# Solve steps queued behind the preceding large matmul, and decay rows loaded and exponentiated later

## The chip, the cores and the metric

The kernel runs on one core of one Trainium2 chip. The metric is the time of one execution on the device in microseconds (us); less is better. Engines: PE (TensorE matmuls; PEld its weight loads), DVE (VectorE), ACT (ScalarE), POOL (GpSimd), and SP (SyncE), which here issues the DMAs.

## The reference

One decoder layer: 512 tokens, width 2048, float32, with two branches side by side. The change concerns the second branch, a gated delta rule with 16 key heads and 32 value heads of 128 numbers each. Cut to what matters:

```python
d_qkv = causal_conv_silu(d_qkv, conv_w)          # 4 taps, per channel
dq, dk = l2_norm(dq), l2_norm(dk)                # per key head
# in chunks of 64 tokens, per value head:
g = jnp.cumsum(g, axis=-1)
decay = jnp.exp(jnp.where(tril, g[..., :, None] - g[..., None, :], -jnp.inf))
L = jnp.where(strict, (k_beta @ k^T) * decay, 0.0)
t_inv = triangular_solve(eye + L, eye)           # 64 x 64, lower
u = t_inv @ v_beta
w = t_inv @ (k_beta * jnp.exp(g)[..., None])
qk = (q @ k^T) * decay
# then a scan over the 8 chunks:
v_new = u_c - w_c @ S
o = qd_c @ S + qk_c @ v_new
S = S * gl_c + kd_c^T @ v_new
```

## The kernel before

**Weights and tiles.** The large projections stream their weights through SBUF as `raw` tiles of 1 MB (two buffers). Each is split by halves into a rounded part `whi` (a cast on ACT, L52) and a rest `wlo` (a subtraction on DVE, L53). A *tile* below is one output tile of 128 channels by 512 tokens: 48 matmuls of 128x512 into one of two PSUM buffers (`mm3`, L223 to L225, called by `channel_tile`). Positions are given in tiles, so tile 29.5 is the middle of tile 29, and a split stands about one half tile ahead of its use at the latest. The branch's tiles come in this order: 0 to 3 merge gates, 4 to 7 keys 4 to 7, 8 to 23 keys 8 to 15 and merge gates in turn, 24 to 30 merge gates, then from 31 on sixteen groups of heads of five tiles each (q, v, v, z, z), group 8 from tile 71.

**Work beside the matmuls.** Everything else of the branch is written as Python generators. After every second k-tile of a channel tile (so eight times per tile) `pump` advances them: the live ones by their delays, and the slow ones by a budget. That is the program order. A scheduler then places the instructions of each engine by its own modelled times, in which the program order is a priority, so an instruction whose operands it takes for ready can stand many tiles ahead of its place in the program. At run time each engine works its list in order and waits at the head of it.

**A key head** (`keys`, two value heads each) runs: convolution (ACT, then three operations on DVE, then tanh `th` on ACT and a product on DVE), transposes `ptk` on PE, sums of squares on ACT (L673), `rsqrt` on DVE in small steps, the norm's products `k` on ACT (L640), transposes `ptkT`, a copy `kT` on ACT (L648), and the key products `pkk` on PE (L655). For each of its two value heads a row block `E` (256 KB, four buffers) is loaded by `decay_load` (L678), masked on POOL (L685, L686), exponentiated on ACT (L650), multiplied with `pkk` on DVE (L658), and stored to `lt_d` and `lab_d`.

**The solves.** `solve` inverts the triangular 64x64 matrices of 16 value heads at once on DVE: solve 0 for the first eight key heads, solve 1 for the others. It loads `A` in two halves of 1 MB and `bet` in two small ones, multiplies `A` by `nbet` (L709), runs 62 steps of two operations each (L717, L723), copies `A` out in four pieces (ACT copy L729, DMA `ta_d` L731), multiplies by `bet` (L733) and stores `ts_d` in two DMAs of 1 MB (L737). In the program solve 0 begins at key 8 and has to end before the first group of heads, solve 1 begins at the first group and ends before group 8. Solve 0's steps are tied in the order behind the latest key's `rsqrt`; solve 1's steps aren't tied to anything.

**A group of heads** (`queries`, `values`, `scan`) loads `E` rows, `kT`, `k`, and blocks of `ts_d`, `ta_d`, `lab_d`, and works through transposes (`ptq`, `ptv`, `pto`), products (`pqk`, `py`, `pu`) and the scan.

Of the kernel before, what the change touches and what calls it, by code (L numbers as in the profile page):

```python
# [2 lines left out]

# [7 lines left out]
AF = mybir.ActivationFunctionType  # L11
# [25 lines left out]
class Layer:  # L37
# [43 lines left out]
    def pump(self):  # L81
        self.weight_tick()
        for e in list(self.live):
            e[1] -= 1
            if e[1] <= 0:
                self.step(e)
        for e in list(self.slow):
            e[2] += e[1]
            while e in self.slow and e[2] >= e[3]:
                e[2] -= e[3]  # L90
                self.step_slow(e)
        for q in list(self.side.values()):
            if not q:
                continue
            q[0][2] += q[0][1]
            while q and q[0][2] >= 1.0:
                q[0][2] -= 1.0
                if next(q[0][0], True):
                    q.pop(0)

    def step(self, e):
        try:
            e[1] = next(e[0]) or 1
        except StopIteration:
            self.live.remove(e)
# [114 lines left out]
    def mm3(self, ps, w, x, first, last):  # L220
        nc = self.nc
        (wh, wl), (xh, xl) = w, x
        nc.tensor.matmul(ps, lhsT=wh, rhs=xh, start=first, stop=False)  # L223
        nc.tensor.matmul(ps, lhsT=wh, rhs=xl, start=False, stop=False)  # L224
        nc.tensor.matmul(ps, lhsT=wl, rhs=xh, start=False, stop=last)  # L225

    def channel_tile(self, name, xh=None, xl=None):

# [395 lines left out]
    def keys(self, wk, g, ps):  # L624

        nc = self.nc
        y = wk.tile([P, T], F32, tag="y", name="y", bufs=3)
        yield from self.conv(wk, ps, 16 + g, y)
        E = [self.decay_load(wk, 2 * g + e) for e in range(2)]
        yield 2  # L630
        pt = self.ptp.tile([P, T], F32, tag="tp", name="ptk")
        self.transpose4(pt, lambda c: y[:, c * P : (c + 1) * P])
        ss = self.sumsq(wk, pt)
        yield 3
        nc.vector.tensor_scalar(out=ss, in0=ss, scalar1=EPS, scalar2=None, op0=ALU.add)
        rk = self.rsqrt(wk, ss, NTB, "rk")
        yield 2
        k = wk.tile([P, NTB, P], F32, tag="k", name="k")
        for c in range(NTB):
            nc.scalar.activation(k[:, c, :], pt[:, c * P : (c + 1) * P], AF.Copy, scale=rk[:, c : c + 1])  # L640
        for e in range(2):
            self.decay_mask(E[e], 2 * g + e)
        yield 3
        pt = self.ptp.tile([P, T], F32, tag="tp", name="ptkT")
        self.transpose4(pt, lambda c: k[:, c, :])
        nc.sync.dma_start(out=self.k_d[g], in_=k.rearrange("p c d -> p (c d)"))
        kT = wk.tile([P, T], F32, tag="kT", name="kT")
        nc.scalar.copy(out=kT, in_=pt)  # L648
        for e in range(2):
            nc.scalar.activation(E[e], E[e], AF.Exp)  # L650
        yield 2
        pk = self.ptp.tile([P, NTB, P], F32, tag="tp", name="pkk")
        for c in range(NTB):
            sl = slice(c * P, (c + 1) * P)
            nc.tensor.matmul(pk[:, c, :], lhsT=kT[:, sl], rhs=kT[:, sl], start=True, stop=True)  # L655
        nc.sync.dma_start(out=self.kT_d[g], in_=kT)
        for e in range(2):
            nc.vector.tensor_tensor(out=E[e], in0=pk, in1=E[e], op=ALU.mult)  # L658
        yield 2
        for e in range(2):  # L660
            h = 2 * g + e
            b, hl = h // 16, h % 16
# [13 lines left out]
    def decay_load(self, wk, h):  # L676
        E = wk.tile([P, NTB, P], F32, tag="E", name="E", bufs=4)
        self.nc.sync.dma_start(out=E.rearrange("p c i -> p (c i)"), in_=self.g_rows[h].partition_broadcast(P))  # L678
        return E
# [840 lines left out]
```

## Time and profile before

| | us |
|---|---|
| median of 3 runs | 2965.86 (2963.03 to 2968.37) |
| profiled execution | 2968.14 |
| its span on the core | 2964.4 |
| PE busy | 2882.8 (97%) |
| DVE busy | 1786.1 (60%) |
| ACT busy | 1086.6 (37%) |
| POOL busy | 236.2 (8%) |

The profile is of one execution. A row of a timeline is: start in us, duration in us, engine, line of the kernel, operation, output and inputs, and in brackets how long the engine had been idle and what ended that. A row of the waits is: who waited, for whom, us in total, times, and the longest. The granted clock of PE is 1.00 at full speed and 0.50 at half.

### The profile page before, as it was taken

What the parts mean: (1) busy time and instruction counts of PE and PEld (TensorE: products, weight loads), DVE (VectorE), ACT (ScalarE), POOL (GpSimd) and SP (SyncE); (2) the same over time, 40 slices, a digit from 0 to 9 for tenths busy, and PEclk for the clock granted to TensorE, in tenths of its full rate; (3) what the DMA queues carried; (4) which work ended last, traced back from release to release, by engine and by line L of the source; (5) the groups of instructions that cost most, each with busy time, mean ns of one, the idle gap of its engine ahead of it and who ended that gap; (6) DMA issues with size and microseconds to landing.
All of it is one profiled execution on the core that took longest, in us unless ns stands there. A gap on an engine that the chain in (4) does not pass through costs nothing.

```text
span 2964.4 us, 38028 instructions
## 1 busy us (share of the span) xinstructions
PE 2882.8 (97%) x14556; PEld 2362.5 (80%) x14556; DVE 1786.1 (60%) x2903; ACT 1086.6 (37%) x2105; POOL 236.2 (8%) x204
## 2 busy tenths in 40 slices
PE   8899999999999999999999999999999999999988
PEld 6687777777888888888888878888788788788877
DVE  7755979998544445454545453433755655554697
ACT  4354433334333333334333322311244434432343
POOL 0012210111000000011000000000100000000013
PEclk9999999999999999999999999999999999999999
DMA  9756555634433333333332575554322223375553
GB/s 382 278 159 189 173 151 156 181 115 123 151 108 122 108 122 115 125 124 116 123 123 86 197 265 193 201 167 162 100 86 98 79 88 107 111 257 174 178 199 96
DMA packets 174023, 451.11 MB, mean 152 GB/s; under 512 B 72177, under 2 KB 74737, under 8 KB 138129
## 3 DMA queue, kind: packets, MB, share of 16 engines
q1 hardware_dynamic: 173842, 448.70, 45.7%
q8 instruction: 114, 1.87, 0.3%
q14 instruction: 67, 0.55, 0.1%
HBM read 386.95 MB, written 59.45 MB: 151 GB/s over the span
## 4 chain that ended last, share of the span: by engine, by line
PE 81%; DVE 9%; DMA 4%; ACT 2%; issue 2%; POOL 1%; SPq 0%; POOLq 0%; DVEq 0%; ACTq 0%
PE mm L223 23%; PE mm L225 22%; PE mm L224 22%; DVE wlo L53 2%; DMA E<-g_rows 1%; DVE wa L396 1%; PE S L1160 1%; PE po L890 1%; PE pv L871 1%; PE O L1211 1%; DVE A L723 1%; PE pP L257 1%; DVE atmp L717 1%; ACT whi L52 1%; PE pd L886 1%
## 5 line engine op out<-in xcount | busy, mean ns | idle before, releaser
L223 PE MATMUL mm<-hh,whi 128*128 128x512 f32 x2784 | 1135.8, 408 | 7.0 <-DVE yq L561 6.2
L225 PE MATMUL mm<-hh,wlo 128*128 128x512 f32 x2784 | 1093.7, 393 | 0.0
L224 PE MATMUL mm<-hl,whi 128*128 128x512 f32 x2784 | 1091.3, 392 | 0.0
L53 DVE TENSOR_TENSOR wlo<-raw,whi 128x1024 fp32r<-128x1024 f32 (+1 forms) x452 | 548.6, 1216 | 491.6 <-ACT whi L52 476.6
L52 ACT CAST whi<-raw 128x1024 fp32r<-128x1024 f32 (+1 forms) x452 | 470.8, 1043 | 951.7 <-PE mm L224 907.0
L223 PEld LDWEIGHTS mm<-hh,whi 128*128 128x128 f32 x2784 | 526.6, 189 | 117.4 <-issue 15.0
L225 PEld LDWEIGHTS mm<-hh,wlo 128*128 128x128 f32 x2784 | 525.5, 189 | 114.3
L224 PEld LDWEIGHTS mm<-hl,whi 128*128 128x128 f32 x2784 | 527.3, 189 | 99.9 <-issue 0.8
L223 PE MATMUL mm<-oh,whi 128*128 128x512 f32 x512 | 200.4, 393 | 1.2 <-ACT whi L52 0.9
L224 PE MATMUL mm<-ol,whi 128*128 128x512 f32 x512 | 199.3, 390 | 0.8 <-DVE ol L53 0.8
L225 PE MATMUL mm<-oh,wlo 128*128 128x512 f32 x512 | 199.4, 390 | 0.5 <-DVE wlo L53 0.5
L818 POOL TENSOR_TENSOR qe<-qe,yq 128x512 f32<-128x512 f32 x32 | 47.3, 1495 | 912.7 <-DMA qe<-eg_rows 848.9
L685 POOL TENSOR_TENSOR E<-E,neg_g 128x512 f32<-128x512 f32 x64 | 76.6, 1197 | 490.9 <-DMA E<-g_rows 427.7
L223 PEld LDWEIGHTS mm<-oh,whi 128*128 128x128 f32 x512 | 96.0, 188 | 23.0 <-ACT whi L52 1.3
L224 PEld LDWEIGHTS mm<-ol,whi 128*128 128x128 f32 x512 | 96.1, 188 | 22.3 <-DVE ol L53 1.2
L225 PEld LDWEIGHTS mm<-oh,wlo 128*128 128x128 f32 x512 | 96.1, 188 | 21.0 <-DVE wlo L53 1.2
L717 DVE TENSOR_TENSOR atmp<-A 128x392 f32<-128x392 f32 (+30 forms) x124 | 108.1, 877 | 2.0
L723 DVE TENSOR_TENSOR A<-A,atmp 128x392 f32<-128x392 f32 (+30 forms) x124 | 108.0, 876 | 2.0
L864 DVE SCALAR_TENSOR_TENSOR r<-pp,neg_eg,vt 128x128 f32<-128x128 f32 x96 | 29.2, 346 | 81.5 <-PE pp L861 79.8
L561 DVE SCALAR_TENSOR_TENSOR yv<-mm,convh,yv 128x511 f32<-128x511 f32 (+2 forms) x96 | 71.3, 743 | 8.2 <-ACT yv L558 6.8
L1184 ACT ACTIVATE sm<-sm,mx,rs 128x256 f32<-128x256 f32 (+1 forms) x128 | 71.7, 562 | 3.3 <-DVE mx L1179 3.3
L224 PE MATMUL m<-wlo,hh 128*128 128x512 f32 x128 | 51.4, 401 | 7.9 <-DVE wlo L53 7.8
(331 smaller groups left out, 3154.9 us busy)
## 6 DMA issues: line engine op xcount, KB each, us to landing
raw<-in_w_ch SPq DMA_DIRECT2D x158, 1024.0 KB
wa<-in_w_ada_ss SPq DMA_DIRECT2D x32, 1024.0 KB
raw<-in_w_od SPq DMA_DIRECT2D x32, 1024.0 KB
E<-g_rows SPq DMA_DIRECT2D x64, 256.0 KB
gw<-in_w_ada_gate SPq DMA_DIRECT2D x16, 1024.0 KB
raw<-in_w_os SPq DMA_DIRECT2D x16, 1024.0 KB
qe<-eg_rows SPq DMA_DIRECT2D x32, 256.0 KB
o_d<-zh SPq DMA_DIRECT2D x32, 256.0 KB
```

Of the source, the lines that this page charges most:

```text
L52: self.nc.scalar.copy(out=hi, in_=src)
L53: self.nc.vector.tensor_tensor(out=lo, in0=src, in1=hi.bitcast(F32), op=ALU.subtract)
L223: nc.tensor.matmul(ps, lhsT=wh, rhs=xh, start=first, stop=False)
L224: nc.tensor.matmul(ps, lhsT=wh, rhs=xl, start=False, stop=False)
L225: nc.tensor.matmul(ps, lhsT=wl, rhs=xh, start=False, stop=last)
L257: self.nc.tensor.transpose(dst[:, c * P : (c + 1) * P], src_cols(c), self.ident)
L561: nc.vector.scalar_tensor_tensor(out=y[:, s:], in0=ps[:, : T - s], scalar=w[:, j : j + 1], in1=y[:, s:], op0=ALU.mult, op1=ALU.add)
L685: nc.gpsimd.tensor_tensor(out=E, in0=E, in1=ng, op=ALU.add)
L717: eng.tensor_tensor(out=t, in0=A[:, m : m + 1, m + 1 :].to_broadcast([P, m, n]), in1=A[:, :m, m : m + 1].to_broadcast([P, m, n]), op=ALU.mult,
L723: eng.tensor_tensor(out=A[:, :m, m + 1 :], in0=A[:, :m, m + 1 :], in1=t, op=ALU.add)
L818: nc.gpsimd.tensor_tensor(out=qf, in0=qf, in1=q, op=ALU.mult)
L1184: nc.scalar.activation(t, t, AF.Exp, scale=r[:, h : h + 1], bias=mx[:, h : h + 1], accum_out=den[:, h : h + 1])
```

## The change

Two things are changed. Every instruction that a solve step issues in `pump` gets an edge to the last large matmul before it in the program, so the scheduler can't place it ahead of that matmul. The edge sets the order only, and no engine waits for it at run time; it holds for a step's DMAs and ACT copies as for its DVE operations. And a key head loads its two `E` blocks after the `rsqrt` is issued instead of after the convolution, and the exps are issued after the key products instead of after the copy `kT`, with one more pump between them and the multiplication.

```diff
     def pump(self):
...
-        for e in list(self.slow):
-            e[2] += e[1]
-            while e in self.slow and e[2] >= e[3]:
-                e[2] -= e[3]
-                self.step_slow(e)
+        with self.behind():
+            for e in list(self.slow):
+                e[2] += e[1]
+                while e in self.slow and e[2] >= e[3]:
+                    e[2] -= e[3]
+                    self.step_slow(e)
...
+    @contextmanager
+    def behind(self):
+
+        n, last = len(self.nc.cur_bb.bb.instructions), self.last_mm
+        yield
+        for i in self.nc.cur_bb.bb.instructions[n:]:
+            self.tc.add_manual_dep(
+                i, last.name, mybir.DependencyInfo(mybir.DependencyClass.NoSync, mybir.DependencyReason.DATA),
+                reason="behind",
+            )
...
-        nc.tensor.matmul(ps, lhsT=wl, rhs=xh, start=False, stop=last)
+        self.last_mm = nc.tensor.matmul(ps, lhsT=wl, rhs=xh, start=False, stop=last).ins
...
     def keys(self, wk, g, ps):
...
         yield from self.conv(wk, ps, 16 + g, y)
-        E = [self.decay_load(wk, 2 * g + e) for e in range(2)]
         yield 2
...
         rk = self.rsqrt(wk, ss, NTB, "rk")
+        E = [self.decay_load(wk, 2 * g + e) for e in range(2)]
         yield 2
...
         nc.scalar.copy(out=kT, in_=pt)
-        for e in range(2):
-            nc.scalar.activation(E[e], E[e], AF.Exp)
         yield 2
...
         nc.sync.dma_start(out=self.kT_d[g], in_=kT)
+        for e in range(2):
+            nc.scalar.activation(E[e], E[e], AF.Exp)
+        yield 1
         for e in range(2):
             nc.vector.tensor_tensor(out=E[e], in0=pk, in1=E[e], op=ALU.mult)
```

Line numbers of the changed kernel are higher by 12 or 13 from here on (L52 and L53 stay). In the order, PE's and POOL's lists are nearly the same as before; those of DVE, ACT and SP move. Three places follow.

DVE before, from the cast of tile 32's second half to the end of the convolutions at tile 33, where the next matmuls wait for `yq` (A and atmp are solve 1's here; solve 0 is over):

```order
L53 TENSOR_TENSOR wlo<-raw,whi 128x1024
L723 TENSOR_TENSOR A<-A,atmp 128x21x42
L717 TENSOR_TENSOR atmp<-A 128x902
L561 SCALAR_TENSOR_TENSOR yq<-mm,convh,yq 128x511
L723 TENSOR_TENSOR A<-A,atmp 128x22x41
L561 SCALAR_TENSOR_TENSOR yq<-mm,convh,yq 128x510
L561 SCALAR_TENSOR_TENSOR yv<-mm,convh,yv 128x511
L561 SCALAR_TENSOR_TENSOR yq<-mm,convh,yq 128x509
```

DVE after, the same place:

```order
L53 TENSOR_TENSOR wlo<-raw,whi 128x1024 x4
L746 TENSOR_TENSOR A<-A,bet 128x4096
L53 TENSOR_TENSOR wlo<-raw,whi 128x1024
L721 TENSOR_SCALAR nbet<-bet 128x64
L573 SCALAR_TENSOR_TENSOR yq<-mm,convh,yq 128x511
L722 TENSOR_TENSOR A<-A,nbet 128x4096
L573 SCALAR_TENSOR_TENSOR yq<-mm,convh,yq 128x510
L723 MEMSET A 128x64
L573 SCALAR_TENSOR_TENSOR yq<-mm,convh,yq 128x509
```

Solve 0's last product (L746) now stands here, at tile 32.2, and was at tile 31.3; solve 1 begins here, with `nbet` and `A` times `nbet` between the operations of `yq`, where before it was at its twenty-second step.

SP before, in the same stretch, from the third piece of solve 0 on (`ta_d`, `ts_d` are solve 0's results):

```order
L731 DMA ta_d<-atmp 64x1024
L183 DMA raw<-in_w_ch 128x2048
L731 DMA ta_d<-atmp 64x1024
L249 DMA ma_d<-mth 128x512
L737 DMA ts_d<-A 64x4096 x2
L183 DMA raw<-in_w_ch 128x2048
L678 DMA E<-g_rows 128x512 x2
L779 DMA kT<-kT_d 128x512
```

SP after:

```order
L712 DMA A<-lt_d 64x4096
L744 DMA ta_d<-atmp 64x1024
L715 DMA bet<-b_rows 64x64
L712 DMA A<-lt_d 64x4096
L744 DMA ta_d<-atmp 64x1024
L750 DMA ts_d<-A 64x4096 x2
L715 DMA bet<-b_rows 64x64
L195 DMA raw<-in_w_ch 128x2048
L691 DMA E<-g_rows 128x512 x2
L792 DMA kT<-kT_d 128x512
```

Solve 1's loads, which stood at tile 2 (`bet`) and at tiles 26 and 27 (`A`), now stand between solve 0's stores, and the second `bet` and the next `raw` stand behind both `ts_d`.

ACT before, at keys 10 and 11 (tiles 14 and 15):

```order
L246 ACTIVATE mth<-mm 128x512
L650 ACTIVATE E<-E 128x512 x2
L640 ACTIVATE k<-ptk,rky 128x128 x4
L52 CAST whi<-raw 128x1024
L650 ACTIVATE E<-E 128x512 x2
L648 COPY kT<-ptkT 128x512
```

ACT after:

```order
L258 ACTIVATE mth<-mm 128x512
L652 ACTIVATE k<-ptk,rky 128x128 x4
L52 CAST whi<-raw 128x1024
L668 ACTIVATE E<-E 128x512 x4
L660 COPY kT<-ptkT 128x512
```

The exps of both keys now stand in one row ahead of the copy `kT`, on which the key products wait, and the products `k` no longer stand behind two of them.

More of the change, by code (lines that the diff above doesn't have):

```diff
@@ L1 @@
 import math
-from contextlib import ExitStack, nullcontext
+from contextlib import ExitStack, contextmanager, nullcontext
 import concourse.bass as bass
```

## The prediction

> **What bounds the kernel now.** I read the page first, then the busy time of each engine by stage, then what PE waits for, and last the timelines around the waits that the change can reach.
>
> ```profile
> span 2964.4 us, 38028 instructions
> PE 2882.8 (97%) x14556; PEld 2362.5 (80%) x14556; DVE 1786.1 (60%) x2903; ACT 1086.6 (37%) x2105; POOL 236.2 (8%) x204
> PE 81%; DVE 9%; DMA 4%; ACT 2%; issue 2%; POOL 1%; SPq 0%; POOLq 0%; DVEq 0%; ACTq 0%
> ```
>
> PE is busy for 2882.8 of 2964.4 us, and it holds 81% of the chain that ended last. The matmuls themselves aren't touched. So the change can only move the 81.6 us in which PE is idle, and the stretches in which PE runs at a lower granted clock. The next view gives, by stage, the window, then the sum, then the busy time of PE, its weight loads, DVE, ACT and POOL, then the granted clock.
>
> ```profile
> 300.00:480.00 180.00, 166.19 (x756) 135.61 (x755) 155.19 (x224) 68.42 (x152) 32.77 (x32) 0.97 0.51 156
> 480.00:720.00 240.00, 230.06 (x1121) 190.55 (x1119) 227.68 (x318) 84.29 (x152) 24.95 (x19) 0.98 0.49 146
> 780.00:1050.00 270.00, 270.00 (x1429) 224.78 (x1428) 134.21 (x253) 100.47 (x224) 24.53 (x24) 1.00 0.37 119
> ```
>
> PE loses 13.8 us while the keys and solve 0 run (DVE 86% busy) and 9.9 us while solve 1 runs (DVE 95% busy). It loses nothing after that (DVE 50% busy). The waits of PE say for what:
>
> ```profile
> PE ptk L257 <- DVE y L568: 11.3, 5, 3.4
> PE ptkT L257 <- ACT k L640: 10.2, 5, 5.5
> PE mm L223 <- DVE yq L561: 6.2, 1, 6.2
> PE pto L257 <- DVE osb L920: 3.9, 2, 3.7
> PE pu L836 <- DMA lab<-lab_d: 2.8, 1, 2.8
> PE ptv L257 <- DVE yv L568: 1.3, 1, 1.3
> ```
>
> The first two are the keys, 21.5 us in ten waits. The third is the hand-over from solve 0 to the heads. The last three (3.9 with a small part elsewhere, 2.8, 1.3) fall beside solve 1. The change reaches these places and no others, and it may open new waits beside them.
>
> **Part 1: the decay rows.** No instruction is added or removed: 32 loads of 256 KB, 32 masks on POOL, 32 exps on ACT. In the order most loads move by a third of a tile or less, since the scheduler had already placed them late. What changes is which ACT work stands behind an exp. Key 6 is the largest wait of this kind (POOL, ACT, PE, then the window behind it):
>
> ```profile
> 254.72 2.10 POOL L685 TENSOR_TENSOR E<-E,neg_g 128x512 f32<-128x512 f32 x1 [5.00 <-DVE y L561]
> 256.90 0.63 POOL L686 TENSOR_SCALAR_AFFINE_SELECT E<-E 128x512 f32<-128x512 f32 x1
> 249.76 0.63 ACT L650 ACTIVATE E<-E 128x512 f32<-128x512 f32 x1 [3.23 <-POOL E L686]
> 257.56 0.63 ACT L650 ACTIVATE E<-E 128x512 f32<-128x512 f32 x1 [5.15 <-POOL E L686]
> 262.59 1.14 ACT L640 ACTIVATE k<-ptk,rky 128x128 f32<-128x128 f32 x4 [2.94 <-DVE rky L64]
> 263.01 1.25 PE L257 MATMUL ptkT<-ident,k 128*128 128x128 f32 x4 [5.47 <-ACT k L640]
> 257.00:275.00 18.00, 12.53 (x56) 10.21 (x55) 10.46 (x28) 10.03 (x24) 4.40 (x5) 0.81 0.46 144
> ```
>
> An exp at 249.76 held back key 6's sums of squares by 3.2 us, and the rsqrt of DVE behind them ended so late that ACT waited another 2.9 us for it. In the new order the sums stand ahead of the exps, and the norm's products stand right behind the exp and th. Counted from the exp at 257.56: 0.6 (exp) + 0.6 (th, an exp's length) + 1.1 (four products) gives about 259.9 against 263.0, so the wait of 5.47 shrinks to about 2.4, a gain of 3.1. The half-speed stretch behind it (18 us at a mean of 0.81, so at most 3.4 us lost, part of which is the idle itself) I take as shortened by 0.9. Of the other 16.0 us of these waits (21.5 less 5.5), keys 9 and 13 to 15 have the same picture with shorter waits; I take a quarter, 4 us. Against that, at keys 10 and 11 the new order puts four exps in a row ahead of the copy kT, on which the key products wait. One mask with its select costs 2.1 + 0.6 us on POOL at worst, so the second key's pair lets kT come about 4 us late where PE waits nearly nothing now. With half clock behind it (1.8), and with key 11's own wait (2.1, one of the five for y) gone, that is 3.7 us lost. The sum is −3.1 − 0.9 − 4 + 3.7, about **−4.5**. The bounds are −11 (all but half of the 21.5 goes) and +4 (only keys 10 and 11 change).
>
> **Part 2: solve 0's end and solve 1's start.** This is the place where tile 33 waits for a free PSUM buffer, which the convolution yq has to read first. Of before, in the order DVE, ACT, SP, POOL, PE:
>
> ```profile
> 530.14 0.26 DVE L723 TENSOR_TENSOR A<-A,atmp 128x62 f32<-128x62 f32 x1
> 548.65 4.43 DVE L733 TENSOR_TENSOR A<-A,bet 128x4096 f32<-128x4096 f32 x1
> 530.44 2.10 ACT L729 COPY atmp<-A 64x1024 f32<-64x1024 f32 x1 [1.24 <-DVE A L723]
> 535.93 2.10 ACT L729 COPY atmp<-A 64x1024 f32<-64x1024 f32 x1 [1.25 <-DMA ta_d<-atmp]
> 555.34 1.05 ACT L52 CAST whi<-raw 128x1024 fp32r<-128x1024 f32 x1 [4.35 <-PE mm L224]
> 560.78 1.06 ACT L52 CAST whi<-raw 128x1024 fp32r<-128x1024 f32 x1 [4.38 <-PE mm L224]
> 553.11 1.09 SPq L737 DMA_DIRECT2D ts_d<-A  x2
> 556.26 0.64 SPq L183 DMA_DIRECT2D raw<-in_w_ch  x1
> 557.00 4.71 SPq L678 DMA_DIRECT2D E<-g_rows  x2
> 564.72 0.32 SPq L779 DMA_DIRECT2D kT<-kT_d  x1
> 569.62 1.82 POOL L685 TENSOR_TENSOR E<-E,neg_g 128x512 f32<-128x512 f32 x1 [104.36 <-DMA E<-g_rows]
> 572.66 0.77 PE L223 MATMUL mm<-hh,whi 128*128 128x512 f32 x1 [6.25 <-DVE yq L561]
> 573.00:576.00 3.00, 3.00 (x8) 2.35 (x8) 3.00 (x5) 0.91 (x2) 2.93 (x3) 0.50 1.14 234
> 303.50 4.42 DVE L709 TENSOR_TENSOR A<-A,nbet 128x4096 f32<-128x4096 f32 x1 [2.77 <-DMA A<-lt_d]
> ```
>
> Solve 0's last step ended at 530.4. Its place in the order moves from tile 29.5 to tile 30.4. The casts at 555.34 and 560.78 belong to tiles 32 and 32.5, half a tile apart, so tile 30.4 is at 560.8 − 2.1 × 10.9 = 538, and the last step ends about there. Each of the four pieces (copy, ta_d) took 5 to 5.5 us; that puts the copies at about 538, 544, 549 and, behind the cast at 555.34 that now stands ahead of it, 556.4 to 558.5. A×bet follows until 562.9, and the two ts_d of 1 MB issue at 563.0 instead of 553.11. On SP the second load of bet (16 KB) now stands directly behind them. On DVE, nbet waits for that load, and behind nbet stand the three yq operations with A×nbet (4.42) and a memset between them. The load's landing is the unknown. Nearest row: the E load issued at 557.00 behind ts_d and a raw had landed only when POOL began at 569.62, 16.5 us after the ts_d issue, and ts_d alone kept SP's load of kT until 564.72, 11.6 us after their issue. So a load behind the two ts_d lands about 11 to 12 us after 563.0, at 574 to 575.3. Then nbet, three yq of 0.7 and A×nbet 4.4 give 7 us: PE starts tile 33 at about 582 against 572.66, **+9.3**. The half clock of the rows at 573 to 576 stands behind both waits and is counted once. The E loads come as much later, and two exps stand ahead of th, which adds at most 3.3 us at the transposes of q; I take 0.7. Sum **+10**. Lower bound: a load that passes the ts_d lands within a few us, and only the order of DVE is left, +1. Upper bound: 9.3 + 3.3 and a raw more in the way, +14. I take the value near the row at 569.62, since both loads are small ones behind the same two stores.
>
> [...]
>
> The two loads of solve 1's A (1 MB each) come into this stretch too, at tiles 31 and 32. They issue before the last ta_d and end before ts_d by the 5.8 us per MB of the two ts_d (11.6 / 2), so they are hidden; without that cover they would add up to a raw's landing, which the upper bound holds.
>
> **Part 3: solve 1 thinned.** Its 62 steps ran beside tiles 27 to 43, and they are now tied to tiles 33 to 60, with the stores at tiles 61 to 66. Its result is read after tile 71, so nothing is late there.
>
> ```profile
> L717 DVE TENSOR_TENSOR atmp<-A 128x392 f32<-128x392 f32 (+30 forms) x124 | 108.1, 877 | 2.0
> 656.00:659.00 3.00, 2.81 (x11) 2.62 (x12) 2.92 (x5) 0.38 (x1) 0.00 (x0) 0.50 0.62 262
> 738.20:743.00 4.80, 4.77 (x25) 3.88 (x26) 4.80 (x2) 2.11 (x3) 0.00 (x0) 0.50 0.33 68
> 728.27 0.48 SPq L731 DMA_DIRECT2D ta_d<-atmp  x1
> 734.74 0.61 SPq L806 DMA_DIRECT2D lab<-lab_d  x1
> 799.28 0.60 PE L257 MATMUL ptv<-ident,yv 128*128 128x128 f32 x4
> 796.91 1.05 DVE L568 SCALAR_TENSOR_TENSOR yv<-th,yv 128x512 f32<-128x512 f32 x1 [2.51 <-ACT th L566]
> ```
>
> A solve costs about 108 us of DVE (L717 for both solves, and the second operation of a step as much again). Over 27 tiles (295 us) that is 37%, on top of the 50% that the heads take alone: 87% instead of 95%. The three waits beside solve 1 cost 3.7 + 2.8 + 1.3 = 7.8 us and half clock for some 3 and 5 us, another 4, so 12 in all. The chain pto (an rsqrt in small DVE steps with solve steps between them) gets half as many steps in its way, and ta_d no longer stands on SP ahead of the lab loads of the same matmul. What remains: in a group without a solve the first ptv starts at 799.28, 1.3 us after its yv is ready (796.91 + 1.05), so one step of 2 × 0.88 us in front of yv makes a wait of about 0.5 us in each of six groups, 3 us; A×bet (4.42) now stands ahead of yv at tile 64.5 and may add 1.5. That makes −12 + 4.5 = **−7.5**, with −12 as the lower end. The upper end is the second rival's, +13.
>
> The sum is −4.5 + 10 − 7.5 = **−2 us**. The profiled run took 2968.14 us (span 2964.4 and 3.7 around it), which is 2.3 above the median of 2965.86. So the run would be at 2966, and the median at about **2964**.
>
> **The rivals.** (a) The load of bet isn't held by the stores: part 2 is +1 and the sum −11, so 2955. The dense DMA after 553 speaks against it, the small size of the load for it. (b) Solve 1 costs in the heads: its steps use up the 1.3 us at the first ptv and more, and each of the six groups waits about 2.4 us. The waits of 2.8, 3.7 and 5.5 us all were followed by half clock, which adds 1.8, so 6 × 4.2 = 25 against the 12 saved: part 3 is +13, the sum +18.5, so 2984. It decides from two or more steps in front of yv. For it speaks that a step follows nearly every half tile there; against it, that in the denser order of before only one of three ptv showed a wait. (c) The new place of the decay rows does nothing, since the scheduler moves them little and the exp still waits for POOL: part 1 is 0, the sum +2.5, 2968.
>
> [...]
>
> **Chances.** Forecast 0.42, (a) 0.16, (b) 0.24, (c) 0.18. About 0.2%, 5.9 us, is what a measurement of this kernel can tell from no change. The forecast's own range is 2956 to 2972, and it splits 0.14 faster, 0.24 same and 0.04 slower. (a) is all faster. (b) is 0.23 slower and 0.01 same. (c) is 0.01 faster, 0.11 same, 0.06 slower. Together: faster 0.31, same 0.36, slower 0.33. The range of 2952 to 2983 takes in (a) and (c) and most of (b).
>
> **What would show it.** Part 1: a wait of ptkT at key 6 of 2 to 2.5 us, and a new wait of pkk at keys 10 and 11 of some 4 us. Part 2: DVE idle in front of nbet at about 563 to 575, "DMA bet", and tile 33's first matmul near 580. Part 3: DVE at 85 to 90% in the heads up to about 870 us, no wait of pu for lab, and waits of ptv under 1 us. The prediction is wrong if DVE doesn't wait at nbet, if ptv or pto wait over 2 us group after group, or if a wait comes up that isn't named here.

## The result, and the profile after

The changed kernel takes 2971.37 us (median of 20 runs, 2963.94 to 2978.9), the kernel before 2968.6 us beside it (20 runs, 2963.03 to 2976.34). The ratio is 1.0009 with an interval of 1.0001 to 1.0016: 0.09% slower, where 0.06% faster was forecast. The time lies in the forecast range and within the 0.2% of "no change", but it went the other way. That small number is a sum of large terms, and each of the three terms of the forecast has another size than forecast.

The profiled run after took 2965.93 us. From its page, the span and the busy times, then the busy time by stage with the columns of the prediction (window, sum, PE, weight loads, DVE, ACT, POOL, granted clock, DMA share, GB/s):

```profile
span 2963.9 us, 38017 instructions
PE 2876.4 (97%) x14556; PEld 2355.0 (79%) x14556; DVE 1793.1 (60%) x2903; ACT 1085.3 (37%) x2105; POOL 240.9 (8%) x204
```

```profile
300.00:480.00 180.00, 175.27 (x810) 143.76 (x809) 161.78 (x233) 69.67 (x147) 34.78 (x32) 0.99 0.48 157
480.00:720.00 240.00, 216.73 (x1058) 178.09 (x1058) 165.86 (x244) 81.28 (x151) 25.82 (x22) 0.95 0.46 139
780.00:1050.00 270.00, 261.83 (x1370) 216.94 (x1369) 181.98 (x299) 102.24 (x212) 26.75 (x24) 0.99 0.37 120
```

PE lost 13.8 us in the first window before and loses 4.7 now. In the second it lost 9.9 and loses 23.3, and the mean clock there falls from 0.98 to 0.95. In the third it lost nothing and loses 8.2. DVE, on the other hand, has become emptier in the second window (227.68 to 165.86 us) and fuller in the third (134.21 to 181.98): solve 1 has moved. What PE waits for from 142 to 1050 us, after (who waits, for whom, us in total, times, longest):

```profile
PE mm L235 <- DVE yq L573: 16.2, 1, 16.2
PE ptv L269 <- DVE yv L580: 7.6, 3, 3.3
PE pto L269 <- DVE osb L933: 5.5, 5, 2.0
PE ptkT L269 <- ACT k L652: 5.4, 4, 1.8
PE ptq L269 <- DVE yq L580: 2.2, 1, 2.2
PE pkk L665 <- ACT kT L660: 0.9, 1, 0.9
PE ptk L269 <- DVE y L580: 0.2, 1, 0.2
```

Of the two waits of the keys, 11.3 and 10.2 us before, the first is nearly gone and the second is halved. The wait at tile 33 has grown from 6.2 to 16.2 us, `ptq` waits there as well, and the heads now wait at `ptv` and `pto`.

To compare kernels by stage I use marks that both have: the same instruction in both, counted from the start. The casts `whi` follow one another at half a tile each, so the n-th cast is the same work in each kernel. The 19th, 73rd, 89th and 149th of the timeline of ACT stand at 142.44, 500.94, 600.61 and 1016.96 us before, and after at:

```profile
142.80 1.04 ACT L52 CAST whi<-raw 128x1024 fp32r<-128x1024 f32 x1
481.38 1.06 ACT L52 CAST whi<-raw 128x1024 fp32r<-128x1024 f32 x1 [4.38 <-DVE atmp L730]
594.80 1.05 ACT L52 CAST whi<-raw 128x1024 fp32r<-128x1024 f32 x1 [0.57 <-PE mm L236]
1016.16 1.05 ACT L52 CAST whi<-raw 128x1024 fp32r<-128x1024 f32 x1
```

The first stretch (19th to 73rd) holds the keys, the second (to the 89th) the hand-over at tile 33, the third (to the 149th) six groups of heads. The keys took 358.50 us before and take 338.58, the hand-over 99.67 and 113.42, the heads 416.35 and 421.36. All kernels of this study by these marks, as differences to the profile before in us (one profile each), with the ratio of their timed runs where there are several:

| kernel | keys | hand-over | heads | sum | ratio [interval] |
|---|---|---|---|---|---|
| before, again | −0.2 | 0.0 | +0.1 | −0.1 | |
| after | −19.9 | +13.7 | +5.0 | −1.2 | 1.0009 [1.0001, 1.0016] |
| after, again | −19.5 | +14.2 | +5.3 | −0.1 | |
| rows only, no ties | −8.7 | +6.5 | −1.4 | −3.6 | 0.9994 [0.9985, 1.0003] |
| ties only, rows as before | −12.6 | +12.1 | +9.0 | +8.4 | 1.003 [1.0019, 1.0041] |
| rows, solve 0 tied | −19.5 | +23.7 | −1.5 | +2.8 | 1.0014 [1.0005, 1.0023] |
| rows, solve 1 tied | −7.0 | +3.8 | +7.6 | +4.4 | 1.0016 [1.0006, 1.0025] |
| after, solve 1's `bet` free | −15.4 | +8.8 | +6.8 | +0.2 | 0.999 [0.9977, 1.0003] |
| after, solve 1's start free | −14.5 | +2.2 | +5.8 | −6.5 | 0.9967 [0.9955, 0.9979] |
| the same, again | −19.0 | +2.6 | +6.0 | −10.5 | 0.997 [0.9957, 0.9982] |
| the same, `th` first in the heads | −20.0 | +4.0 | +2.7 | −13.3 | 0.9961 [0.9948, 0.9975] |
| after, `th` first in the heads | −19.4 | +11.8 | +1.9 | −5.7 | 0.9989 [0.998, 0.9998] |
| after, solve 1 cut to one step | −20.3 | +12.9 | −12.5 | −19.9 | 0.9943 [0.9929, 0.9956] |

(Five more variants of "solve 1's start free" stand below.) So the change gains 20 us at the keys, and the next two stages take it back. The sum by the marks and the median don't agree to the microsecond: after, it is −1.2 and −0.1 by the marks and about +2.7 by the ratio; in the other kernels the two differ by up to 6 us. The rest of the program behind the 149th cast, which the change doesn't touch, took 1947.4 and 1951.4 us in the two profiles before and 1947.7 and 1951.2 in the two after (and up to 1955.9 in other kernels). One profile against another can't show 3 us there, so it isn't located where the remaining 3 us come from.

### The profile page after: what moved, and what is told of

It reads as the page before. It is cut to its first block, busy times and chain, and to the rows that moved or that the text cites. A ratio compares the mean times of both kernels' runs of the same rounds, so it can differ in the third digit from the quotient of the medians.

```text
span 2963.9 us, 38017 instructions
## 1 busy us (share of the span) xinstructions
PE 2876.4 (97%) x14556; PEld 2355.0 (79%) x14556; DVE 1793.1 (60%) x2903; ACT 1085.3 (37%) x2105; POOL 240.9 (8%) x204
## 4 chain that ended last, share of the span: by engine, by line
PE 79%; DVE 9%; DMA 5%; ACT 3%; issue 2%; POOL 1%; SPq 0%; POOLq 0%; DVEq 0%; ACTq 0%
PE mm L235 22%; PE mm L237 22%; PE mm L236 22%; DVE wlo L53 2%; DVE wa L408 1%; PE S L1173 1%; PE pv L884 1%; PE po L903 1%; DMA E<-g_rows 1%; PE O L1224 1%; PE pP L269 1%; DMA bet<-b_rows 1%; ACT whi L52 1%; DVE atmp L730 1%; PE po L902 1%
## 5 line engine op out<-in xcount | busy, mean ns | idle before, releaser
L235 PE MATMUL mm<-hh,whi 128*128 128x512 f32 x2784 | 1132.7, 407 | 16.9 <-DVE yq L573 16.2
L53 DVE TENSOR_TENSOR wlo<-raw,whi 128x1024 fp32r<-128x1024 f32 (+1 forms) x452 | 551.1, 1221 | 517.5 <-ACT whi L52 502.7
L52 ACT CAST whi<-raw 128x1024 fp32r<-128x1024 f32 (+1 forms) x452 | 470.8, 1043 | 971.6 <-PE mm L236 909.3
L730 DVE TENSOR_TENSOR atmp<-A 128x62 f32<-128x62 f32 (+30 forms) x124 | 112.9, 910 | 1.0
L736 DVE TENSOR_TENSOR A<-A,atmp 128x62 f32<-128x62 f32 (+30 forms) x124 | 109.2, 881 | 2.3
```

What stands on the lines that cost most here:

```text
L52: self.nc.scalar.copy(out=hi, in_=src)
L53: self.nc.vector.tensor_tensor(out=lo, in0=src, in1=hi.bitcast(F32), op=ALU.subtract)
L730: eng.tensor_tensor(out=t, in0=A[:, m : m + 1, m + 1 :].to_broadcast([P, m, n]), in1=A[:, :m, m : m + 1].to_broadcast([P, m, n]), op=ALU.mult,
L736: eng.tensor_tensor(out=A[:, :m, m + 1 :], in0=A[:, :m, m + 1 :], in1=t, op=ALU.add)
```

## The experiments

Three theories stood at the start. For the keys: the gain comes from the rows (the forecast's part 1), or from the tie of solve 0's steps, which the forecast had costed only at the solve's end. For the hand-over: `bet` behind the stores, or the fuller DVE. For the heads: solve 1's steps cost per step, or per group. The line numbers are those of each kernel and lie up to 15 higher or 1 lower than in the changed one.

### Which part does what

Rows only. The tie is taken out of `pump`:

```diff
-        with self.behind():
-            for e in list(self.slow):
-                e[2] += e[1]
-                ...
+        for e in list(self.slow):
+            e[2] += e[1]
+            ...
```

> Decay rows moved, solve steps not tied. Theory 'rows' (the 19.6 us that tile 33 gained by the start of its wait come from the new place of the decay rows): tile 33's wait starts 17 to 20 us earlier than before, the hand-over wait and the stage of solve 1 stay as before, and the whole is 15 to 20 us faster (ratio about 0.994). Theory 'ties' (the gain comes from solve 0's steps being tied, which thins DVE's list beside the keys): tile 33's wait starts at most 5 us earlier, ratio 0.998 to 1.000.

Ties only. The loads and exps of the rows stand where they stood before:

```diff
         yield from self.conv(wk, ps, 16 + g, y)
+        E = [self.decay_load(wk, 2 * g + e) for e in range(2)]
...
-        E = [self.decay_load(wk, 2 * g + e) for e in range(2)]
...
         nc.scalar.copy(out=kT, in_=pt)
+        for e in range(2):
+            nc.scalar.activation(E[e], E[e], AF.Exp)
```

> Solve steps tied, decay rows as before. Theory 'rows': nothing gained at the keys, the hand-over wait of 16 us and the waits beside solve 1 as in the changed kernel, so about 15 to 19 us slower (ratio 1.005 to 1.0065). Theory 'ties': the keys gain 15 us or more, ratio about 1.000 to 1.001.

Rows with only solve 0 tied, and with only solve 1 tied (`e[1]` is the pace, 0.5 for solve 1 alone; the second kernel has `==` in place of `!=`):

```diff
-        with self.behind():
-            for e in list(self.slow):
+        for e in list(self.slow):
+            with self.behind() if e[1] != 0.5 else nullcontext():
```

> Decay rows moved, solve 0 tied, solve 1 free. If the hand-over wait comes from solve 1's loads and first steps standing behind solve 0's stores (theory 'bet behind the stores'), it falls from 16.2 us to 7 or less, since those loads are early again, and the groups of heads after 780 us lose nothing: 12 to 18 us faster than before (ratio about 0.995). If it comes from solve 0 ending late (theory 'late end'), a wait of 10 us or more stays at tile 33.

> Decay rows moved, solve 1 tied, solve 0 free. Here solve 1's loads of A stand behind solve 0's stores, but the convolution yq stands ahead of nbet on DVE. 'Bet behind the stores': tile 33 starts without a long wait, yet the split of the next half, which stands behind A times nbet, waits instead: 3 to 10 us lost there. The groups of heads up to 950 us lose about 17 us as in the changed kernel, against 12 before. Whole: 5 to 12 us faster (ratio 0.996 to 0.998).

Measured: the four lines of the table. At the keys, the rows alone gain 8.7 us, the ties alone 12.6, both 19.9. Of the ties it is solve 0's: with solve 0 tied the keys gain 19.5, with solve 1 tied 7.0, no more than with none. As wholes the four came out otherwise than expected: both theories for the keys hold in part, and the two kernels with one tie, which were to be 12 to 18 us (if `bet` alone made the wait) and 5 to 12 us faster than before, are 0.14% and 0.16% slower. The waits of PE from 142 to 523 us say how, first of the rows only, then of the ties only:

```profile
PE ptk L268 <- DVE y L579: 9.4, 4, 3.8
PE pkk L664 <- ACT kT L659: 3.2, 1, 3.2
PE ptkT L268 <- ACT k L651: 2.0, 2, 1.0
```

```profile
PE ptkT L269 <- ACT k L652: 8.9, 6, 3.2
PE ptk L269 <- DVE y L580: 1.5, 3, 1.0
PE pkk L667 <- ACT kT L660: 0.7, 1, 0.7
```

Before, `ptk` waited 11.3 us for `y` and `ptkT` 10.2 us for `k`. The rows take away the waits for `k` (10.2 to 2.0), which is the mechanism of the forecast; the ties take away those for `y` (11.3 to 1.5). What made a `y` late can be read in the timeline of DVE of the kernel before, ahead of the wait of 3.41 us of `ptk` at 408.67:

```profile
404.96 0.74 DVE L561 SCALAR_TENSOR_TENSOR y<-mm,convh,y 128x509 f32<-128x509 f32 x1
405.62 1.17 DVE L717 TENSOR_TENSOR atmp<-A 128x980 f32<-128x980 f32 x1
406.71 1.22 DVE L53 TENSOR_TENSOR wlo<-raw,whi 128x1024 fp32r<-128x1024 f32 x1
407.84 0.68 DVE L568 SCALAR_TENSOR_TENSOR y<-th,y 128x512 f32<-128x512 f32 x1
```

Half a step of solve 0 (L717) and a split stand between the convolution and the product that `ptk` needs. Four more halves, the last from 400.23 to 401.40, stand between ACT's part of the convolution (395.62) and its first operation on DVE (401.32). Those ahead are the ones that the tie thins out, not those behind: after, at the same key, one half stands ahead of that operation and two behind it. Counted from ACT's part to the product, keys 13 to 15 have 5, 4 and 5 halves in the way before, 5, 7 and 2 with the rows only, 3, 3 and 3 with the ties only and 3, 3 and 2 after. The time from the one to the other is 12.2, 10.5 and 12.1 us before and 9.3, 8.0 and 8.3 us after.

The hand-over waits without `bet` too. In the rows-only kernel solve 1 isn't tied and `bet` loads early, and yet tile 33 waits 11.85 us; with solve 0 tied and solve 1 free it waits 26.60 us. The first matmul of tile 33, then the window ahead of it, of the kernel with solve 0 tied:

```profile
573.06 0.77 PE L235 MATMUL mm<-hh,whi 128*128 128x512 f32 x1 [26.60 <-DVE yq L573]
530.00:570.00 40.00, 16.46 (x73) 13.31 (x71) 37.07 (x34) 13.78 (x11) 4.62 (x3) 0.74 0.62 167
```

The matmul starts at 573.06, 0.4 us from where it started before (572.66). PE comes 19.5 us earlier out of the keys, and DVE, whose list is full with steps of solve 1 and splits ahead of `yq` (37.07 of 40 us busy), doesn't. So an untied solve 1 gives the gain of the keys back at tile 33 without any help of `bet`.

### The hand-over taken apart

After, in the order SP, DVE, ACT, PE, and two windows behind the first matmul:

```profile
543.75 1.10 SPq L750 DMA_DIRECT2D ts_d<-A  x2
544.90 2.68 SPq L715 DMA_DIRECT2D bet<-b_rows  x1
547.62 2.27 SPq L195 DMA_DIRECT2D raw<-in_w_ch  x1
556.25 0.20 DVE L721 TENSOR_SCALAR nbet<-bet 128x64 f32<-128x64 f32 x1 [11.40 <-DMA bet<-b_rows]
559.64 1.05 ACT L52 CAST whi<-raw 128x1024 fp32r<-128x1024 f32 x1 [12.07 <-DMA raw<-in_w_ch]
565.68 0.63 ACT L825 ACTIVATE E<-E 128x512 f32<-128x512 f32 x1 [1.96 <-POOL E L699]
566.21 0.61 ACT L578 ACTIVATE th<-yq 128x512 f32<-128x512 f32 x1
563.03 0.76 PE L235 MATMUL mm<-hh,whi 128*128 128x512 f32 x1 [16.18 <-DVE yq L573]
563.00:567.00 4.00, 2.47 (x5) 1.48 (x5) 2.29 (x3) 1.78 (x3) 2.57 (x3) 0.50 1.03 236
567.00:572.00 5.00, 4.30 (x13) 3.56 (x14) 4.88 (x10) 1.88 (x9) 2.52 (x2) 0.50 0.62 170
```

DVE stands idle for 11.40 us in front of `nbet`, as forecast: `bet`, 16 KB, was issued behind the two stores of 1 MB and is there 12.5 us after the first of them (543.75 to 556.25). ACT stands idle for 12.07 us too, for the `raw` behind `bet`. The 2.2 us of `ptq` (at 567.70) have another cause: its `th` stands right behind the second exp, which waits for POOL, and POOL could begin only at 560.89, when the `E` rows behind the same stores had landed. With that exp tied behind `th` (the last kernel under "The heads") `ptq` waits 0.84 us. Two kernels free `bet`, alone and with everything that solve 1 does before its first step (the loads of `A` and `bet`, `nbet`, `A` times `nbet`, the memset), by leaving these instructions out of the tie:

```diff
+    @contextmanager
+    def untied(self, free):
+        n = len(self.nc.cur_bb.bb.instructions)
+        yield
+        if free:
+            self.loose.update(i.name for i in self.nc.cur_bb.bb.instructions[n:])
...
         for i in self.nc.cur_bb.bb.instructions[n:]:
+            if i.name in self.loose:
+                continue
...
+            with self.untied(b == 1):
                 nc.sync.dma_start(out=bet[s], ...)
```

> The changed kernel, with only solve 1's two small loads of bet freed from the tie, so that they stand early in SP's list as before the change. 'Bet behind the stores': DVE's idle time of 11.4 us in front of nbet goes, and the wait at tile 33 falls from 16.2 us to 5 to 8 (A times nbet still stands ahead of yq), so 8 to 11 us faster than the changed kernel up to the middle of the heads. 'Late end' (solve 0's stores themselves hold PE): the wait stays above 12 us.

> The changed kernel, with solve 1's loads, nbet and A times nbet freed from the tie and its 62 steps still tied. If the hand-over costs 13.7 us only by what stands ahead of yq on DVE, the wait at tile 33 falls to about 3 us, and the whole is 10 to 13 us faster than the changed kernel: 7 to 12 us faster than before (ratio 0.996 to 0.9975). If PE's earlier arrival is always given back at this place, the wait stays above 10 us and the ratio at 1.000.

Measured, the waits of PE at the hand-over, and the cast of ACT, with `bet` free:

```profile
PE ptq L279 <- DVE yq L590: 8.2, 1, 8.2
PE mm L245 <- DVE yq L583: 6.4, 1, 6.4
564.47 1.04 ACT L53 CAST whi<-raw 128x1024 fp32r<-128x1024 f32 x1 [12.25 <-DMA raw<-in_w_ch]
```

and with the whole start free:

```profile
PE mm L245 <- DVE yq L583: 5.5, 1, 5.5
```

With `bet` free the matmul waits 6.4 us instead of 16.2, but the next thing behind the same stores comes to the fore: the `raw`, whose cast ACT has at the head of its list, ahead of the `th` that `ptq` needs. With the whole start free, the `ptq` wait is gone as well, and the hand-over costs 2.2 us instead of 13.7. That kernel takes 0.9967 of the time before [0.9955, 0.9979], and again 0.997 [0.9957, 0.9982]: faster than both kernels.

> The best version so far once more, beside the two others on the same chip: 0.9967 again, inside 0.9955 to 0.9979, heads +5.8, waits of ptv 8.0 us and of pto 5.5 us.

Its two profiles differ by 4.5 us at the keys (−14.5 and −19.0) and by at most 0.4 at the two other stages, so a difference at the keys of that size says little in one profile.

### The heads

Solve 1 without 61 of its 62 steps, everything else as after:

```diff
+            if b == 1 and m > 1:
+                continue
             yield 0.2 + 0.0023 * m * n
```

> The changed kernel without 61 of solve 1's 62 steps (so the heads of the second half get a wrong inverse); loads, products, copies and stores stay. 'Solve 1 costs in the heads': the 17.5 us that the groups of heads lose between 590 and 950 us go (under 3 us left), the hand-over wait of 16 us stays, and the whole is about 17 us faster than the changed kernel (ratio to before 0.995). If the losses come from the DMAs or from the ACT copies of solve 1, most of them stay.

Measured: the heads take 403.85 us (416.35 − 12.5), PE waits neither for `ptv` nor for `pto`, and the ratio is 0.9943. Against that, the kernel before loses 12.5 us beside solve 1 and the kernel after 17.5. The kernel after, timeline of PE: the waits of the second to the fifth group, and then a window behind each (the first group waits 0.42 us for `pto` and 1.97 for `ptv`, and 0.65 and 0.62 us follow on the first two rows here):

```profile
713.46 0.66 PE L269 MATMUL pto<-ident,osb 128*128 128x128 f32 x4 [1.86 <-DVE osb L933]
783.79 0.66 PE L269 MATMUL pto<-ident,osb 128*128 128x128 f32 x4 [1.96 <-DVE osb L933]
861.66 0.41 PE L269 MATMUL ptv<-ident,yv 128*128 128x128 f32 x2 [3.28 <-DVE yv L580]
933.05 0.41 PE L269 MATMUL ptv<-ident,yv 128*128 128x128 f32 x2 [2.31 <-DVE yv L580]
711.00:720.00 9.00, 6.49 (x34) 4.91 (x33) 9.00 (x12) 2.73 (x4) 4.20 (x5) 1.00 0.16 58
785.00:790.00 5.00, 4.66 (x17) 3.93 (x18) 5.00 (x7) 2.08 (x3) 0.69 (x1) 0.71 0.29 107
861.00:866.00 5.00, 4.34 (x19) 3.95 (x20) 3.71 (x5) 2.22 (x3) 0.00 (x0) 0.70 0.61 210
933.00:938.00 5.00, 4.95 (x28) 4.32 (x29) 4.41 (x6) 2.35 (x4) 0.00 (x0) 1.00 0.53 162
```

In five of six groups PE waits 2.3 to 3.3 us, 13.1 us together (7.6 and 5.5 in the waits above). The other 4.4 us are slower work: between the two marks PE is busy for 408.3 us, and for 403.85 without the steps. Half clock behind two of the waits, 0.29 of 5 us and 0.30 of 5 us, makes 3 of them. To tell a price per step from a price per group, the pace of solve 1 was doubled and was lowered, both in the kernel with the start free:

```diff
-                s1 = self.paced(self.solve(sol1, 1, nc.vector), 0.5)
+                s1 = self.paced(self.solve(sol1, 1, nc.vector), 1.0)
```

> Solve 1's start freed as in e6, and its pace doubled from 0.5 to 1.0, so its steps lie in three groups of heads instead of five or six, twice as dense. If a group loses by the number of steps that stand in front of its pto and ptv (theory 'per step'), three groups lose 5 to 7 us each, as in the kernel before, 15 or more in all. If it loses once for having a solve beside it (theory 'per group'), three groups lose 2.5 to 5 each, 7 to 12 in all. The hand-over has some ten short steps ahead of yq, so its wait grows by 3 to 8 us over e6's 5.5.

(The other has 0.4 in the same place.)

> As e6, with solve 1's pace lowered from 0.5 to 0.4, so its steps lie in seven groups of heads, a fifth thinner. 'Per step': a group loses less (the first ones under 2 us) and the whole is 0 to 5 us faster than e6. 'Per group': two more groups lose 2.5 us or more each, and the whole is 3 to 6 us slower than e6.

Measured at the heads: +4.2 at double pace (0.9967 [0.9955, 0.9979]), +5.8 at the pace of the change, +12.6 and 1.7 more in the two groups behind the 149th cast at the slow one (0.9992 [0.9983, 1.0002]). Against the heads without steps that is 16.7, 18.3 and 25.1 us. Neither theory holds by itself. Per step, the three would be equal; per group, double pace would cost half. At double pace `pto` waits 3.0 to 3.7 us in three groups. The slow one is dearest: each of its five waits of `ptv` (15.5 us in all) is 2.5 to 3.5 us long, and the mean clock over the 12 or 13 us from each is 0.76 to 0.87. Why its waits are that long isn't shown.

Why `ptv` waits at all shows on ACT. After, ahead of the wait of 3.28 us at 861, then the same place in the fourth group of the kernel without solve 1's steps, where `ptv` doesn't wait:

```profile
856.36 0.63 ACT L825 ACTIVATE E<-E 128x512 f32<-128x512 f32 x1 [6.64 <-POOL E L699]
858.09 0.63 ACT L825 ACTIVATE E<-E 128x512 f32<-128x512 f32 x1 [1.10 <-POOL E L699]
858.62 1.03 ACT L52 CAST whi<-raw 128x1024 fp32r<-128x1024 f32 x1
859.56 0.63 ACT L578 ACTIVATE th<-yv 128x512 f32<-128x512 f32 x1
```

```profile
843.54 0.63 ACT L827 ACTIVATE E<-E 128x512 f32<-128x512 f32 x1 [4.97 <-POOL E L699]
844.08 0.61 ACT L578 ACTIVATE th<-yv 128x512 f32<-128x512 f32 x1
845.27 0.64 ACT L827 ACTIVATE E<-E 128x512 f32<-128x512 f32 x1 [0.57 <-POOL E L699]
```

Where there are no steps, `th` stands behind one exp, in all six groups. In the five groups that wait after, it stands behind both and, in two of them, behind a cast as well. Two kernels tie the second exp behind `th` in the order, one with the start free and one as the changed kernel:

```diff
-        for e in range(2):
-            nc.scalar.activation(M[e], M[e], AF.Exp)
+        nc.scalar.activation(M[0], M[0], AF.Exp)
+        self.tc.add_manual_dep(
+            nc.scalar.activation(M[1], M[1], AF.Exp).ins, self.last_th.name,
+            mybir.DependencyInfo(mybir.DependencyClass.NoSync, mybir.DependencyReason.DATA), reason="th first",
+        )
```

> The best version so far, and in each group of heads the second exp of the decay rows is tied in the order behind the th of the first value tile. Theory 1: the waits of ptv come from ACT, where th stands behind both exps (and a cast), which wait for POOL; in groups without solve steps th stands between the exps and ptv doesn't wait. Then the waits of ptv (8.0 us in four groups, and the half clock behind some) go, the waits of pto (5.5 us) stay, and the heads' stage falls from +5.8 to about -4 against before, the ratio by about 0.002 to 0.003 to 0.994 to 0.995. Theory 2: the steps on DVE in front of yv make the waits, and the place of th doesn't matter. Then ptv still waits 6 us or more, and the stage stays within 2 us of +5.8.

> The changed kernel with the same tie of the second exp behind th. Theory 1: the waits of ptv (7.6 us in three groups, two of them 1.97 and 2.31, one of 3.28 with half clock behind it) go, those of pto stay; the heads' stage falls from +5.0 to about -4, the keys and the hand-over stay at -20 and +14, and the ratio falls from 1.0009 to about 0.998. Theory 2: ptv waits as before, the ratio stays at 1.000 to 1.001.

Measured: the heads fall to +2.7 and +1.9, by 3.2 and 3.1 us (from 5.95 and 5.01), a third of the 9 to 10 that theory 1 asks for. In the changed kernel the three waits of `ptv` go from 1.97, 3.28 and 2.31 to 1.14, 1.56 and 2.10; a fourth of 0.73 comes up, and `pto` goes from 5.5 to 5.9. So the place of `th` is a part. The steps on DVE, theory 2, are another, which is read here in one group. DVE of that kernel ahead of the wait of 2.10 us at 927.39, with `th` ready at 924.72:

```profile
923.55 1.51 DVE L736 TENSOR_TENSOR A<-A,atmp 128x486 f32<-128x486 f32 x1
924.99 1.65 DVE L53 TENSOR_TENSOR wlo<-raw,whi 128x1024 fp32r<-128x1024 f32 x1
926.56 0.68 DVE L580 SCALAR_TENSOR_TENSOR yv<-th,yv 128x512 f32<-128x512 f32 x1
```

Half a step and the split behind it hold `yv` back until 926.56. With the start free and `th` first, the ratio is 0.9961 [0.9948, 0.9975], the lowest of all kernels here that compute the whole; against 0.997 of the same without that tie, on the same chip, the intervals overlap. For the changed kernel it is 0.9989 [0.998, 0.9998] against 1.0009 [1.0001, 1.0016].

### The decay rows by halves

In the kernel with solve 1's start free: the rows as before; then only the loads late (the exps stay behind the copy `kT`); then only the exps late (the loads stay behind the convolution). The diffs are the lines of "ties only", whole and by halves.

> Solve steps tied with solve 1's start freed, as in e6, but the decay rows loaded and exponentiated as before the change. If the rows add to what the tie of solve 0 gains at the keys, tile 33's wait starts 4 us or more later than in e6 and the ratio is 0.998 to 0.999. If the tie alone does it, it is as e6 within 2 us (0.9967).

> As e6, but only the loads of the decay rows are issued later; the exps stand after the copy kT as before the change. 'Loads': the gain that the rows add at the keys (about 5 us over e10) stays, and tile 33's wait starts at about 552; the new wait of pkk at keys 10 and 11 stays too, since four exps still stand ahead of one copy kT. 'Exps': it starts 4 us or more later, as in e10 (557).

> As e6, but only the exps are issued later; the loads stand after the convolution as before the change. 'Loads': tile 33's wait starts at about 557, as in e10, and the wait of 5.4 us at key 6 is back. 'Exps': it starts at 552 or earlier. No wait of pkk over 1 us at keys 10 and 11, since ACT has two exps ahead of k and two ahead of kT there, as before.

| start free, and | keys | hand-over | heads | sum | ratio [interval] |
|---|---|---|---|---|---|
| rows as before | −9.5 | +0.4 | +5.2 | −3.9 | 0.9989 [0.9979, 0.9998] |
| only the loads late | −16.2 | +1.5 | +8.9 | −5.9 | 0.9977 [0.9966, 0.9988] |
| only the exps late | −14.9 | +2.2 | +5.9 | −6.8 | 0.9987 [0.9977, 0.9997] |
| double pace | −16.0 | +8.0 | +4.2 | −3.8 | 0.9967 [0.9955, 0.9979] |
| slow pace | −20.0 | +3.6 | +12.6 | −3.8 | 0.9992 [0.9983, 1.0002] |

Either half gains 5 to 7 us at the keys over the rows as before, each in one profile; both together gain 5.0 and 9.5 in the two profiles of that kernel. The halves don't add up, and with a scatter of 4.5 us at this stage their order isn't shown. The times say little more: both together (0.9967, and again 0.997) lie below the rows as before (0.9989), but the intervals touch or overlap, and those of either half overlap both.

### The two kernels once more

> The changed kernel once more, for a second trace. If the account by stage is stable, the start of tile 33's wait, the wait itself and the losses in the heads repeat within 1 us each, and what differs from the first trace lies before 140 us and after 1700 us.

> The kernel before once more, for a second trace: the waits at the keys, at tile 33 (6.2 us) and beside solve 1 (12.5 us lost by 780 us) repeat within 1 us each, if the account by stage is stable.

Measured: 2970.51 and 2968.89 us, and the first and third lines of the table: each profile repeats its stages within 0.5 us, the heads and the hand-over included. For these two kernels the differences by stage are their own; the 4.5 us between the two profiles with the start free shows that this doesn't hold for every kernel at the keys. Only one wait was clearly another: `pkk` at keys 10 and 11 waits 0.87 us in the first profile after and 3.36 in the second.

## Why the prediction was right or wrong

**Part 1, the decay rows: −4.5 forecast, −19.9 measured, outside the bound of −11.** (The forecast's own terms add up to −4.3.) The failing step is "Of the other 16.0 us of these waits", where "keys 9 and 13 to 15 have the same picture" and "I take a quarter, 4 us". None of the four has that picture in the trace before: no exp stands in the way. At key 9, `k` waited for an rsqrt that stood on DVE behind `A` times `nbet` of solve 0 (303.50 to 307.92) and among its steps. At keys 13 to 15, ACT was idle for 3.0 to 3.7 us ahead of `th`, for DVE's convolution. So the step looked for these waits in the rows, and put the effect of solve 0's tie on them at nothing, costing it only where the solve ends, in part 2. By "rows only" the rows gain 8.7 us, twice the forecast. The other 11 come with the tie, which takes steps of solve 0 out of the way of `y`. The five waits for `y` stood in the prediction's own row (11.3 us), in a stretch that it said was 86% DVE, and it didn't ask what stands ahead of `y` on DVE. Key 6's wait, forecast to shrink from 5.47 to 2.4 us, went altogether; the second exp, which the forecast left at 257.56, ran at 253.13. A wait of 1.59 us came up at key 7. From 250 to 275 us the clock is 1.00 where it was 0.86. The new wait of `pkk` at keys 10 and 11 came, with 0.9 and 3.4 us after and 2.5 to 5.3 in all but one of the other kernels that have both the loads and the exps late, where about 4 was forecast.

**Part 2, the hand-over: +10 forecast, +13.7 measured, inside the bound of +14.** The mechanism is the forecast one: DVE idle in front of `nbet`, for `bet`, behind the two stores. The wait, forecast as 6.25 + 9.3 = 15.6, is 16.18 us, and `bet` landed 12.5 us after the stores' issue, where 11 to 12 was forecast. Mis-sized are two smaller terms. `ptq`, taken as 0.7, is 2.2 us, by the two exps ahead of its `th` that the forecast named; and the half clock, "counted once" with its old length, lasts from 563.0 to about 573 us (0.50 to 572, 0.89 from 572 to 576) instead of from 572.7 to about 577 (0.50 from 573 to 576, 0.85 from 576 to 580). What is left for it is 13.75 − 9.93 − 2.20 = 1.6 us, and half of the some 3.2 us more in which PE worked at half clock is as much. Rival (a), that the stores don't hold `bet`, is out; the `raw` behind `bet` came 15.9 us after their issue (543.75 to 559.64). How they hold the loads isn't shown. The forecast had solve 0's last product in the way at 558.5 to 562.9; it ran at 539.30, 19 us earlier, since the keys had gained that; the wait behind it has the forecast length all the same, since the stores and `bet` came as much earlier.

**Part 3, the heads: −7.5 forecast, +5.0 measured, inside its bounds.** Rival (b) had the mechanism: waits in group after group with half clock behind some. The failing step is "one step … in front of yv makes a wait of about 0.5 us in each of six groups": 4.5 us were to remain, and 17.5 remain. The waits are 2.3 to 3.3 us in five groups. The forecast put one step on DVE into a row from a group without a solve (the first `ptv` 1.3 us behind its `yv`) and left everything else in its place. But with the steps in the list, `th` also stands behind a second exp and sometimes a cast on ACT, and that exp waits for POOL (1.10 us ahead of the wait at 861). And `osb` waits for an rsqrt in small DVE steps, which the forecast expected to get half as many solve steps in its way. One is enough: in the second group the chain from `ms` to `osb` takes 9.1 us (703.66 to 712.72), with one step in it and, behind that step, a split and three operations of `yv`; without steps it takes 2.6 us (699.66 to 702.27) and is over before that split. Rival (b) in turn priced half clock behind each wait, at 1.8 us, and it came behind two of them, with about 1.5 us each.

**The sum.** −19.9 + 13.7 + 5.0 is −1.2 where −2 was forecast: that the sums are so close is luck, by misses of −15.4, +3.7 and +12.5 that cancel. The timed runs went the other way, to 0.09% slower (about +2.7 us), and where these last us lie stays open. The kernel with only the ties (1.003) and the one with the start free (0.9967) show what was in it either way.

## What to carry to other kernels

A tie in the order acts wherever the tied work had stood before and wherever it stands then: cost it at each stage, and on each list that it is inserted into, ACT's included. A gain at one stage is worth what the next one lets through; here PE's 20 us at the keys ran into the first list that doesn't follow, a small load behind large stores (16.2 us) or a full DVE (26.6 us). So free the start of the moved work, loads and first products, from the tie, and keep the tie for its many steps.

## What the runs showed of the hardware

**Half clock came behind short waits, and not always.** After, the pair of waits at 713 (1.86 and 0.65 us) leaves the clock at 1.00; the pair at 784 (1.96 and 0.62) is followed by 0.71 from 785 to 790. Behind 2.31 us at 933 the clock is 1.00. In the kernel before, 2.28 us at key 9 is followed by a mean of 0.68 over the next 4 us. The same wait went both ways: behind 3.28 us at 861 the next 4 us have 0.67, and behind the same wait of 3.27 us in the second profile of this kernel they have 1.00. In the 19 profiles of this study, from 200 to 1100 us, the clock over the 4 us from the end of a wait of PE was below 0.95 behind 18 of 47 waits of 1.5 to 2.0 us, behind 40 of 53 of 2.0 to 3.27 us, and behind all 49 that were longer. Of these, the profiles of before and after have 2 of 7, 4 of 6 and 6 of 6. What decides behind which of the short waits the clock falls isn't shown.

**Issues took longer right behind the two large stores.** After, SP took 2.68 us to issue `bet` (16 KB) and 2.27 us for a `raw` (1 MB), right behind the two stores; a `raw` further on took 0.69 us (555.83) or 0.33 us (860.94). With `bet` free, the `raw` that then stands first behind the stores took 2.65 us, so here it is the place and not the size. In the kernel before, a `raw` 2.1 us behind the stores' issue took 0.64 us (556.26), and the two `E` behind it 4.71 us together.

**POOL was slower while DVE worked on solve steps.** In the heads after (640 to 940 us) the products `qe` take 1685 ns on average, the sums of `E` 1269 and the selects 826; in the groups without a solve of the kernel before (800 to 1050 us) it is 1478, 1050 and 635. From 600 to 1050 us it is 1640, 1232 and 795 after, and 1587, 1046 and 635 with solve 1's steps taken out of the changed kernel. The sums and the selects are what the exps wait for. How the steps slow POOL isn't shown. No run here takes POOL's part of the waits away by itself.
